# Two hybrid decoder layers on one Trainium2 core: high parts first in each weight half, and plain fp32 for the first pair of projections and the last down projections

## The chip, the core and the metric

The kernel runs on one core of a Trainium2 chip. The metric is the device time of one execution in microseconds. Besides the timed runs there is one profiled execution, from which every row below comes.

## What is computed

Two decoder layers work on 256 tokens of 1024 channels. Each layer projects `x` to 6,144 and more columns, runs three mixers on them (an RWKV-7 recurrence, a Conformer convolution, a short gated convolution), merges them with sigmoid gates, projects back and normalises. The first layer then has a dense SwiGLU, the second one a top-2-of-8 expert SwiGLU. Cut to what matters:

```python
p = x @ w_in                                   # all mixers' inputs and the gates
x = layernorm(alpha * x + (g_a*y_a + g_b*y_b + g_c*y_c) @ w_out)
f = (silu(x @ w_gate) * (x @ w_up)) @ w_down   # layer 0
...
yb = (silu(xs @ w_gate[e]) * (xs @ w_up[e])) @ w_down[e]   # layer 1, rows of expert e
x = layernorm(alpha * x + f)
```

## The kernel before

All weights come as 1 MB units of 128 partitions x 2048 fp32 columns, loaded on SyncE's queue (`fetch`, line 174) into a ring of buffers. Each unit is used in two halves of 1024 columns. `split` (line 197) makes two fp32r tiles of a half: ScalarE casts the high part `hi` (line 205), then VectorE subtracts it from the source to give the low part `lo` (line 207). Both tiles come from pools that turn round: three slots, to which a stage can add six.

A product is then made of several TensorE matmuls that add up in one PSUM tile. `mm3` (line 215) makes three of them: high x high (line 217), high x low (line 218) and low x high (line 219). `mm2` (line 1407) makes two, for experts whose rows are few: there the high and low parts of 64 rows lie side by side in one stationary tile, so `hi` (line 1408) and `lo` (line 1409) of the weights each need one pass.

In `proj` (line 360) the weights are stationary and `x` moves, 256 columns at a time, eight k-tiles to a half, so 24 matmuls. In the expert stage (`moe`, line 1190) the gathered rows are stationary and the weights move, 512 columns at a time. A half of a large expert then has two k-tiles (or, in a down projection, two output halves) and six matmuls, a half of a small one four. The four experts with most rows are `big`, with up to 128 rows, the other four are small, with up to 64. They run as two streams of steps `(r, j)`, rank `r` and 256 hidden columns `j` (0 to 10), in turn. A step has four halves of gate and up (`kind` 0) and, two steps later, two halves of the down projection (`kind` 1). The last two down steps of all are those of `(3, 10)` and `(7, 10)`. After the last down step of an expert, `scatter` (line 1309) casts and splits the result and adds it to the tokens by a one-hot matmul.

In the expert stage the order of TensorE, VectorE, ScalarE and SyncE is the order in which the program is written: for each half a cast, a subtraction, the matmuls, and then whatever is due from a list `later` (hidden activations, transposes, gathers, scatters). Everywhere else the compiler's scheduler orders the engines' queues.

At the start (`start`, line 340) unit 0 comes in two halves with `x` between them, `x` is split too (lines 356 and 357), and the first projected pair holds the inputs of the low-rank chain (`lora_part`, line 437): ScalarE shifts (line 428), tanh, sigmoids, exponentials. The mixer's own chain of small operations runs on VectorE and ScalarE, while `fill` (line 766) keeps TensorE in work with the other projections.

The kernel has matmuls on plain fp32 operands as well, in the mixer (lines 448, 459, 493). Each stands as two matmuls in the trace.

Of the kernel before, what the change touches and what calls it, by code (L numbers as in the profile page):

```python
# [11 lines left out]
F32 = mybir.dt.float32  # L12
F32R = mybir.dt.float32r
BF16 = mybir.dt.bfloat16
# [8 lines left out]
T = 256  # L23
# [25 lines left out]
BUSY = 7, 2, 4  # L49
LAG = 2  # L50
CONV_AT = 7
SPLITS = 3, 4, 0, 0, 3
# [91 lines left out]
class Net:  # L144
# [69 lines left out]

    def mm3(self, out, lh, ll, rh, rl, start, stop):
        mm = self.nc.tensor.matmul
        mm(out, lhsT=lh, rhs=rh, start=start, stop=False)  # L217
        mm(out, lhsT=lh, rhs=rl, start=False, stop=False)  # L218
        return mm(out, lhsT=ll, rhs=rh, start=False, stop=stop)  # L219

# [119 lines left out]
    def start(self):  # L340
        nc, A = self.nc, self.A
        raw = self.ring.tile([128, 2048], F32, name="raw")
        w = A["wst"][0]
        self.unit = 1
        with self.tc.tile_pool(name="xin", bufs=1) as xp:
            xf = xp.tile([128, 8, T], F32, name="xf")
            nc.sync.dma_start(raw[:, 0:1024], w[:, 0:1024])
            for g in range(2):
                nc.sync.dma_start(xf[:, 4 * g:4 * g + 4], A["xT"][:, 4 * g:4 * g + 4])
            nc.sync.dma_start(raw[:, 1024:2048], w[:, 1024:2048])  # L350
            self.first = [self.split(raw[:, 0:1024])]
            self.xTh = self.act.tile([128, 8, T], F32R, name="xTh")
            self.xTl = self.act.tile([128, 8, T], F32R, name="xTl")
            for g in range(2):
                s = slice(4 * g, 4 * g + 4)
                nc.scalar.copy(self.xTh[:, s], xf[:, s])  # L356
                nc.vector.tensor_sub(self.xTl[:, s], xf[:, s], self.xTh[:, s])  # L357
            self.first.append(self.split(raw[:, 1024:2048]))

    def proj(self, region, hl):  # L360
        hi, lo = hl
        for k in range(8):
            s = slice(k * 128, (k + 1) * 128)
            self.mm3(region, hi[:, s], lo[:, s], self.xTh[:, k], self.xTl[:, k], k == 0, k == 7)

    def by_token(self, hls, m):
        ps, n = self.pa(), 8 // len(hls)
        w, t = 1024 // n, slice(m * 128, (m + 1) * 128)
        for k in range(8):
            (hi, lo), s = hls[k // n], slice(k % n * w, (k % n + 1) * w)  # L370
            ins = self.mm3(ps[:, 0:w], self.xTh[:, k, t], self.xTl[:, k, t], hi[:, s], lo[:, s], k == 0, k == 7)
        return ps, ins
# [20 lines left out]

    def proj2(self):
        ps = self.pa()
        first, self.first = self.first, None
        for c, hl in enumerate(first or self.halves()):
            self.proj(ps[:, c * 256:(c + 1) * 256], hl)
        return ps
# [366 lines left out]
    def fill(self, l):  # L766
# [3 lines left out]
        with tc.tile_pool(name="fl", bufs=1) as W:  # L770
# [28 lines left out]
            for o in (yc, self.ybc):  # L799
# [4 lines left out]
                for hn, (hi, lo) in enumerate(self.halves()):  # L804
                    for n in range(0, 4, 2):
                        ps = self.pa()
                        for j in range(2):
                            for k in range(2):
                                s = slice(((n + j) * 2 + k) * 128, ((n + j) * 2 + k + 1) * 128)
                                self.mm3(ps[:, j * T:(j + 1) * T], hi[:, s], lo[:, s], yh[:, k], yl[:, k], k == 0, k == 1)  # L810
# [42 lines left out]
    def merge(self, l):  # L853
# [3 lines left out]
        for g in range(2):  # L857
            raw = self.fetch()
            for hn in range(2):
# [3 lines left out]
                for j in range(2):  # L863
                    for k in range(4):
                        s = slice((j * 4 + k) * 128, (j * 4 + k + 1) * 128)
                        self.mm3(ps[:, j * T:(j + 1) * T], hi[:, s], lo[:, s], self.yah[:, k], self.yal[:, k],
                                 k == 0, k == 3)
                s = slice(n, n + 2)
# [15 lines left out]
    def out_mm(self, lh, ll, hl, m, k, last, ns=(0, 1)):  # L884
        for n in ns:
            s = slice(n * 512, (n + 1) * 512)
            self.mm3(self.acc[2 * m + n], lh, ll, hl[0][:, s], hl[1][:, s], k == 0, k == last)

# [301 lines left out]
    def moe(self, W):  # L1190
# [33 lines left out]
        def due(t):  # L1224
            while True:
# [41 lines left out]
        def hidden_big(r, j, ps):  # L1267
# [4 lines left out]
            def turned():  # L1272
# [4 lines left out]

                def split():
                    hh = W.tile([128, 2, 128], F32R, name="hh", bufs=2)
# [7 lines left out]
        def hidden_small(r, j, ps):  # L1287
# [8 lines left out]
            def act():  # L1296
# [3 lines left out]

                def split():
                    hh = W.tile([128, 2, 128], F32R, name="hh", bufs=2)
                    nc.scalar.copy(hh[:, :, 0:64], sg)
# [30 lines left out]
        def product(kind, rj, i, hl):  # L1334
            r, j = rj
            big = r < BIG
            hi, lo = hl
            if kind == 0:
                if i == 0:
                    gps[rj] = self.pa()  # L1340
                ps = gps[rj]
                for kk in range(2):
                    k, s = 2 * i + kk, slice(kk * 512, (kk + 1) * 512)
                    if big:
                        self.mm3(ps, xe[r][:, 0, k], xe[r][:, 1, k], hi[:, s], lo[:, s], k == 0, k == 7)
                    else:
                        self.mm2(ps, xe[r][:, k], hi[:, s], lo[:, s], k == 0, k == 7)
                if i == 3:
                    del gps[rj]
                    at(4, lambda: (hidden_big if big else hidden_small)(r, j, ps))  # L1350
            else:
# [4 lines left out]
                if r not in Y:  # L1356
                    Y[r] = [self.pb(), self.pb()]
                for n in range(2):
                    s = slice(n * 512, (n + 1) * 512)
                    first, last = j == 0 and i == 0, j == NJ - 1 and i == 1  # L1360
                    h = hid[rj]
                    if big:
                        self.mm3(Y[r][n], h[0][:, i], h[1][:, i], hi[:, s], lo[:, s], first, last)
                    else:
                        self.mm2(Y[r][n], h[0][:, i], hi[:, s], lo[:, s], first, last)
                if i == 1:
# [39 lines left out]

    def mm2(self, out, l, rh, rl, start, stop):
        self.nc.tensor.matmul(out, lhsT=l, rhs=rh, start=start, stop=False)  # L1408
        self.nc.tensor.matmul(out, lhsT=l, rhs=rl, start=False, stop=stop)  # L1409

# [167 lines left out]
```

## Time and profile before

| | us |
|---|---|
| median of 3 runs (lowest, highest) | 1465.1 (1461.07, 1465.63) |
| profiled execution, its own time | 1463.08 |
| its span | 1461.3 |
| TensorE matmuls busy | 1405.8 |
| VectorE busy | 1223.5 |
| ScalarE busy | 970.0 |

The span is the time from the first to the last instruction of the profiled execution, the other 1.8 us lie around it. PE is TensorE's matmuls, PEld its weight loads, DVE VectorE, ACT ScalarE, POOL GpSimd. A matmul's recorded time includes waiting behind the one before it, so neighbouring matmuls overlap in the timeline; their pace is the distance between starts.

### The profile page before, as it was taken

What the parts mean: (1) busy time and instruction counts of PE and PEld (TensorE: products, weight loads), DVE (VectorE), ACT (ScalarE), POOL (GpSimd) and SP (SyncE); (2) the same over time, 40 slices, a digit from 0 to 9 for tenths busy, and PEclk for the clock granted to TensorE, in tenths of its full rate; (3) what the DMA queues carried; (4) which work ended last, traced back from release to release, by engine and by line L of the source; (5) the groups of instructions that cost most, each with busy time, mean ns of one, the idle gap of its engine ahead of it and who ended that gap; (6) DMA issues with size and microseconds to landing.
All of it is one profiled execution on the core that took longest, in us unless ns stands there. A gap on an engine that the chain in (4) does not pass through costs nothing.

```text
span 1461.3 us, 24189 instructions
## 1 busy us (share of the span) xinstructions
PE 1405.8 (96%) x9375; PEld 1202.3 (82%) x9377; DVE 1223.5 (84%) x1651; ACT 970.0 (66%) x1378; POOL 37.9 (3%) x72
## 2 busy tenths in 40 slices
PE   7999999999999999999999999999999999999994
PEld 6989898899997989999877887688876888768882
DVE  6799687755546799677789999999999999999997
ACT  7554564544435645464589888788887888878883
POOL 0030000000000030000000000000000000000000
PEclk9999999999999999999999999999999999999998
DMA  6334355655432424356389999899998999989990
GB/s 225 140 130 160 117 205 202 230 209 193 176 128 100 161 104 157 120 185 276 148 303 372 411 418 408 330 383 377 422 408 330 365 402 420 399 330 407 417 402 31
DMA packets 55640, 390.80 MB, mean 267 GB/s; under 512 B 6192, under 2 KB 6192, under 8 KB 9568
## 3 DMA queue, kind: packets, MB, share of 16 engines
q1 hardware_dynamic: 53136, 381.18, 67.0%
q0 software_dynamic: 2096, 7.49, 1.5%
q8 instruction: 75, 1.23, 0.3%
q10 hardware_dynamic: 288, 0.52, 0.1%
q14 instruction: 45, 0.37, 0.1%
HBM read 387.08 MB, written 2.10 MB: 266 GB/s over the span
## 4 chain that ended last, share of the span: by engine, by line
PE 79%; DVE 14%; ACT 3%; issue 3%; DMA 0%; ACTq 0%; DVEq 0%; POOLq 0%
PE pa L217 14%; PE pa L218 14%; PE pa L219 14%; DVE lo L207 7%; PE pb L218 5%; PE pb L219 5%; PE pb L217 5%; PE pa L1409 4%; PE pa L1408 4%; PE pa L1292 2%; PE pb L1409 2%; PE pb L1408 2%; ACT hi L205 2%; PE pb L627 1%; DVE ybc L230 1%
## 5 line engine op out<-in xcount | busy, mean ns | idle before, releaser
L207 DVE TENSOR_TENSOR lo<-raw,hi 128x1024 fp32r<-128x1024 f32 x648 | 775.5, 1229 | 126.8 <-ACT hi L205 125.8
L205 ACT CAST hi<-raw 128x1024 fp32r<-128x1024 f32 x648 | 656.3, 1052 | 175.9 <-PE pa L218 139.5
L217 PE MATMUL pa<-xTh,hi 128*128 128x256 f32 x1072 | 308.4, 288 | 7.3 <-ACT xTh L356 7.3
L219 PE MATMUL pa<-xTh,lo 128*128 128x256 f32 x1072 | 306.2, 286 | 6.1 <-DVE lo L207 6.1
L218 PE MATMUL pa<-xTl,hi 128*128 128x256 f32 x1072 | 304.6, 284 | 2.3 <-DVE xTl L357 2.3
L217 PEld LDWEIGHTS pa<-xTh,hi 128*128 128x128 f32 x1072 | 205.4, 192 | 11.8 <-ACT xTh L356 7.3
L219 PEld LDWEIGHTS pa<-xTh,lo 128*128 128x128 f32 x1072 | 205.4, 192 | 10.1 <-DVE lo L207 8.5
L218 PEld LDWEIGHTS pa<-xTl,hi 128*128 128x128 f32 x1072 | 205.9, 192 | 3.2 <-DVE xTl L357 2.6
L218 PE MATMUL pa<-lo,xeb 128*128 128x512 f32 x352 | 142.9, 406 | 4.1 <-DVE lo L207 3.2
L217 PE MATMUL pa<-hi,xeb 128*128 128x512 f32 x352 | 144.5, 410 | 0.0
L1408 PE MATMUL pa<-hi,xes 128*128 128x512 f32 x352 | 143.5, 408 | 0.7 <-ACT hi L205 0.7
L1409 PE MATMUL pa<-lo,xes 128*128 128x512 f32 x352 | 140.8, 400 | 2.9 <-DVE lo L207 2.9
L219 PE MATMUL pa<-hi,xeb 128*128 128x512 f32 x352 | 140.0, 398 | 0.0
L218 PE MATMUL pb<-lo,hh 128*128 128x512 f32 x264 | 105.2, 398 | 1.5 <-DVE lo L207 1.5
L217 PE MATMUL pb<-hi,hh 128*128 128x512 f32 x264 | 104.7, 397 | 0.0
L219 PE MATMUL pb<-hi,hl 128*128 128x512 f32 x264 | 104.4, 395 | 0.0
L207 DVE TENSOR_TENSOR lo<-ga,hi 128x1024 fp32r<-128x1024 f32 x74 | 88.3, 1222 | 3.7 <-ACT hi L205 3.7
L218 PEld LDWEIGHTS pa<-lo,xeb 128*128 128x128 f32 x352 | 66.9, 190 | 28.0 <-DVE lo L207 14.2
L1409 PEld LDWEIGHTS pa<-lo,xes 128*128 128x128 f32 x352 | 66.4, 189 | 21.8 <-DVE lo L207 8.8
L219 PEld LDWEIGHTS pa<-hi,xeb 128*128 128x128 f32 x352 | 66.8, 190 | 13.9
L217 PEld LDWEIGHTS pa<-hi,xeb 128*128 128x128 f32 x352 | 67.0, 190 | 13.5
L1408 PEld LDWEIGHTS pa<-hi,xes 128*128 128x128 f32 x352 | 66.3, 188 | 13.7 <-ACT hi L205 1.4
(394 smaller groups left out, 1993.4 us busy)
## 6 DMA issues: line engine op xcount, KB each, us to landing
raw<-in_wst SPq DMA_DIRECT2D x322, 1024.0 KB, 6.7
ga<-in_wst SPq DMA_DIRECT2D x37, 1024.0 KB, 7.1
raw<-in_wst SPq DMA_DIRECT2D x4, 512.0 KB, 6.7
xf<-in_xT SPq DMA_DIRECT2D x2, 512.0 KB, 5.6
raw<-in_lora SPq DMA_DIRECT2D x2, 512.0 KB, 5.5
kk<-in_lnp POOLq DMA_DIRECT2D x2, 512.0 KB, 4.0
v<-in_lnp POOLq DMA_DIRECT2D x2, 512.0 KB, 5.7
xsave<-ga POOLq DMA_DIRECT2D x2, 512.0 KB, 3.6
```

Of the source, the lines that this page charges most:

```text
L205: self.nc.scalar.copy(hi, src)
L207: self.nc.vector.tensor_sub(lo, src, hi)
L217: mm(out, lhsT=lh, rhs=rh, start=start, stop=False)
L218: mm(out, lhsT=lh, rhs=rl, start=False, stop=False)
L219: return mm(out, lhsT=ll, rhs=rh, start=False, stop=stop)
L230: return self.nc.vector.scalar_tensor_tensor(out, a, s, b, op0=op0, op1=op1)
L627: ins = nc.tensor.matmul(ps[s, n * 64:(n + 1) * 64], lhsT=lhsT[s, 8 * b + n], rhs=rhs[s, 8 * b + n], start=True, stop=True)
L1292: nc.tensor.matmul(pt[:, f * 64:(f + 1) * 64], lhsT=gu[:, f * 128:(f + 1) * 128], rhs=self.fold, start=True, stop=True)
L1408: self.nc.tensor.matmul(out, lhsT=l, rhs=rh, start=start, stop=False)
L1409: self.nc.tensor.matmul(out, lhsT=l, rhs=rl, start=False, stop=stop)
```

## The change

`mm3` and `mm2` take a list of products instead of one. For the whole list they first issue every matmul that reads the `hi` part of the weights, and then every one that reads `lo`. `moving` tells whether the weights are the moving or the stationary operand. `proj` gives its eight k-tiles as one list, the expert stage the two k-tiles or output halves of a half, and the merge, the branch outputs and `by_token` their lists alike.

The first pair of projections is not split any more: 16 plain fp32 matmuls read the loaded tiles. Fifteen matmuls on zeros (`WARM`) stand in front of them. The down projections of `(3, 10)` and `(7, 10)` are plain fp32 too, four matmuls of 512 columns each, without a cast and a subtraction of their weights.

```diff
+WARM = 15
-    def mm3(self, out, lh, ll, rh, rl, start, stop):
+    def mm3(self, items, moving):
         mm = self.nc.tensor.matmul
-        mm(out, lhsT=lh, rhs=rh, start=start, stop=False)
-        mm(out, lhsT=lh, rhs=rl, start=False, stop=False)
-        return mm(out, lhsT=ll, rhs=rh, start=False, stop=stop)
+        for out, lh, ll, rh, rl, start, _ in items:
+            mm(out, lhsT=lh, rhs=rh, start=start, stop=False)
+            if moving:
+                mm(out, lhsT=ll, rhs=rh, start=False, stop=False)
+            else:
+                mm(out, lhsT=lh, rhs=rl, start=False, stop=False)
+        for out, lh, ll, rh, rl, _, stop in items:
+            if moving:
+                ins = mm(out, lhsT=lh, rhs=rl, start=False, stop=stop)
+            else:
+                ins = mm(out, lhsT=ll, rhs=rh, start=False, stop=stop)
+        return ins
...
+            zero = xp.tile([128, 512], BF16, name="z")
+            nc.vector.memset(zero, 0.0)
+            ps = self.pa()
+            for _ in range(WARM):
+                nc.tensor.matmul(ps, lhsT=zero[:, 0:128], rhs=zero, start=True, stop=True)
...
-            self.first = [self.split(raw[:, 0:1024])]
+            ps = self.first = self.pa()
+            for c in range(2):
+                for k in range(8):
+                    s = slice(c * 1024 + k * 128, c * 1024 + (k + 1) * 128)
+                    nc.tensor.matmul(ps[:, c * T:(c + 1) * T], lhsT=raw[:, s], rhs=xf[:, k], start=k == 0, stop=k == 7)
...
-            self.first.append(self.split(raw[:, 1024:2048]))
...
+        plain = [(r, NJ - 1) for r in (BIG - 1, NE - 1)]
...
+                    if (r, j) in plain:
+                        hh = W.tile([128, 2, 128], F32, name="hh", bufs=2)
+                        nc.gpsimd.memset(hh[:, :, 64:128], 0.0)
+                        nc.scalar.copy(hh[:, :, 0:64], sg)
+                        hid[r, j] = (hh,)
+                        return
...
+                if lo is None:
+                    for n, s in ns:
+                        nc.tensor.matmul(Y[r][n], lhsT=h[0][:, i], rhs=hi[:, s], start=first, stop=last)
+                elif big:
+                    self.mm3([(Y[r][n], h[0][:, i], h[1][:, i], hi[:, s], lo[:, s], first, last)
+                              for n, s in ns], True)
+                else:
+                    self.mm2([(Y[r][n], h[0][:, i], hi[:, s], lo[:, s], first, last) for n, s in ns])
...
-                hl = self.split(raw[:, h * 1024:(h + 1) * 1024])
-                product(kind, rj, i, hl)
+                part = raw[:, h * 1024:(h + 1) * 1024]
+                product(kind, rj, i, (part,) if kind and rj in plain else self.split(part))
...
+    def mm2(self, items):
+        for out, l, rh, rl, start, _ in items:
+            self.nc.tensor.matmul(out, lhsT=l, rhs=rh, start=start, stop=False)
+        for out, l, rh, rl, _, stop in items:
+            self.nc.tensor.matmul(out, lhsT=l, rhs=rl, start=False, stop=stop)
```

## Rows read from the trace of the kernel before

**Rows 1.** The page: span, and busy time of the engines.

```profile
span 1461.3 us, 24189 instructions
...
PE 1405.8 (96%) x9375; PEld 1202.3 (82%) x9377; DVE 1223.5 (84%) x1651; ACT 970.0 (66%) x1378; POOL 37.9 (3%) x72
```

**Rows 2.** Waits: who waited for whom, us in total, times, longest us.

```profile
ACT hi L205 <- PE pa L218: 139.5, 77, 4.0
...
PE pb L1409 <- DVE lo L207: 6.4, 9, 2.1
PE pa L219 <- DVE lo L207: 6.1, 8, 1.6
PE pa L218 <- DVE lo L207: 3.2, 10, 0.4
PE pa L1409 <- DVE lo L207: 2.9, 5, 0.8
PE pb L218 <- DVE lo L207: 1.5, 3, 0.8
```

**Rows 3.** Windows of the expert stage: length, busy PE, PEld, DVE, ACT, POOL; clock, DMA.

```profile
820.00:895.00 75.00, 75.00 (x347) 61.15 (x347) 73.58 (x80) 64.84 (x85) 0.00 (x0) 1.00 1.01 415
896.00:1000.00 104.00, 100.66 (x466) 78.68 (x464) 97.05 (x113) 83.08 (x121) 0.00 (x0) 1.00 0.95 366
```

**Rows 4.** The chain that ended last, first 64 us: start, us, what.

```profile
10.14 0.58 PE pa L218
...
13.71 0.21 PE pa L218
...
17.57 0.12 PE pa L218
...
57.78 1.82 PE pb L493 x8
```

**Rows 5.** ScalarE's timeline of the start: start, us, line, operation, [idle before <-releaser].

```profile
6.18 1.04 ACT L356 CAST xTh<-xf 128x1024 fp32r<-128x1024 f32 x1 [0.42 <-DMA xf<-in_xT]
...
9.34 1.04 ACT L205 CAST hi<-raw 128x1024 fp32r<-128x1024 f32 x1 [0.27 <-DMA raw<-in_wst]
...
13.13 1.05 ACT L205 CAST hi<-raw 128x1024 fp32r<-128x1024 f32 x1 [2.74 <-DMA raw<-in_wst]
...
17.84 0.47 ACT L428 ACTIVATE sh<-pa,par 128x255 f32<-128x255 f32 x1 [1.95 <-PE pa L219]
...
29.30 1.03 ACT L205 CAST hi<-raw 128x1024 fp32r<-128x1024 f32 x1
```

**Rows 6.** Timeline of the mixer in layer 0, around its last wait for lo.

```profile
108.15 1.05 ACT L205 CAST hi<-raw 128x1024 fp32r<-128x1024 f32 x1
...
110.72 0.38 PE L219 MATMUL pa<-xTh,lo 128*128 128x256 f32 x1 [0.97 <-DVE lo L207]
```

**Rows 7.** TensorE's timeline in the expert stage, at the first change of experts.

```profile
946.36 0.39 PE L217 MATMUL pa<-hi,xeb 128*128 128x512 f32 x1
947.02 0.50 PE L218 MATMUL pa<-lo,xeb 128*128 128x512 f32 x1 [0.28 <-DVE lo L207]
947.36 0.39 PE L219 MATMUL pa<-hi,xeb 128*128 128x512 f32 x1
947.59 0.40 PE L217 MATMUL pa<-hi,xeb 128*128 128x512 f32 x1
```

**Rows 8.** Timeline of the last down projections and scatters.

```profile
1432.34 0.39 PE L217 MATMUL pb<-hi,hh 128*128 128x512 f32 x1
...
1436.13 0.40 PE L219 MATMUL pb<-hi,hl 128*128 128x512 f32 x1
...
1439.16 0.40 PE L1408 MATMUL pb<-hi,hh 128*128 128x512 f32 x1
1441.69 0.50 PE L1409 MATMUL pb<-lo,hh 128*128 128x512 f32 x1 [2.14 <-DVE lo L207]
1443.37 1.07 ACT L1316 CAST yh<-pb 128x512 fp32r<-128x512 f32 x2 [4.32 <-PE pb L1409]
```

More of the change, by code (lines that the diff above doesn't have):

```diff
@@ L357, in start @@
                 nc.vector.tensor_sub(self.xTl[:, s], xf[:, s], self.xTh[:, s])
-            self.first.append(self.split(raw[:, 1024:2048]))
     def proj(self, region, hl):
         hi, lo = hl
-        for k in range(8):
-            s = slice(k * 128, (k + 1) * 128)
-            self.mm3(region, hi[:, s], lo[:, s], self.xTh[:, k], self.xTl[:, k], k == 0, k == 7)
+        cols = [slice(k * 128, (k + 1) * 128) for k in range(8)]
+        self.mm3([(region, hi[:, s], lo[:, s], self.xTh[:, k], self.xTl[:, k], k == 0, k == 7)
+                  for k, s in enumerate(cols)], False)
     def by_token(self, hls, m):
@@ L368, in by_token @@
         w, t = 1024 // n, slice(m * 128, (m + 1) * 128)
-        for k in range(8):
-            (hi, lo), s = hls[k // n], slice(k % n * w, (k % n + 1) * w)
-            ins = self.mm3(ps[:, 0:w], self.xTh[:, k, t], self.xTl[:, k, t], hi[:, s], lo[:, s], k == 0, k == 7)
+        for h, (hi, lo) in enumerate(hls):
+            ins = self.mm3([(ps[:, 0:w], self.xTh[:, h * n + i, t], self.xTl[:, h * n + i, t],
+                             hi[:, i * w:(i + 1) * w], lo[:, i * w:(i + 1) * w], h + i == 0, h * n + i == 7)
+                            for i in range(n)], True)
         return ps, ins
@@ L394, in proj2 @@
     def proj2(self):
+        first, self.first = self.first, None
+        if first is not None:
+            return first
         ps = self.pa()
-        first, self.first = self.first, None
-        for c, hl in enumerate(first or self.halves()):
+        for c, hl in enumerate(self.halves()):
             self.proj(ps[:, c * 256:(c + 1) * 256], hl)
@@ L807, in fill @@
                         for j in range(2):
-                            for k in range(2):
-                                s = slice(((n + j) * 2 + k) * 128, ((n + j) * 2 + k + 1) * 128)
-                                self.mm3(ps[:, j * T:(j + 1) * T], hi[:, s], lo[:, s], yh[:, k], yl[:, k], k == 0, k == 1)
+                            w = [slice(((n + j) * 2 + k) * 128, ((n + j) * 2 + k + 1) * 128) for k in range(2)]
+                            self.mm3([(ps[:, j * T:(j + 1) * T], hi[:, s], lo[:, s], yh[:, k], yl[:, k], k == 0, k == 1)
+                                      for k, s in enumerate(w)], False)
                         r = o[:, 4 * hn + n:4 * hn + n + 2].rearrange("p a t -> p (a t)")
@@ L863, in merge @@
                 for j in range(2):
[L864 to L867, printed above, removed]
+                    w = [slice((j * 4 + k) * 128, (j * 4 + k + 1) * 128) for k in range(4)]
+                    self.mm3([(ps[:, j * T:(j + 1) * T], hi[:, s], lo[:, s], self.yah[:, k], self.yal[:, k],
+                               k == 0, k == 3) for k, s in enumerate(w)], False)
                 s = slice(n, n + 2)
@@ L884, in out_mm @@
     def out_mm(self, lh, ll, hl, m, k, last, ns=(0, 1)):
-        for n in ns:
-            s = slice(n * 512, (n + 1) * 512)
-            self.mm3(self.acc[2 * m + n], lh, ll, hl[0][:, s], hl[1][:, s], k == 0, k == last)
+        cols = [slice(n * 512, (n + 1) * 512) for n in ns]
+        self.mm3([(self.acc[2 * m + n], lh, ll, hl[0][:, s], hl[1][:, s], k == 0, k == last)
+                  for n, s in zip(ns, cols)], True)
     def ln_rows(self, idx, pool, names=("lnG", "lnB")):
@@ L1301, in split @@
                 def split():
+                    if (r, j) in plain:
+                        hh = W.tile([128, 2, 128], F32, name="hh", bufs=2)
+                        nc.gpsimd.memset(hh[:, :, 64:128], 0.0)
+                        nc.scalar.copy(hh[:, :, 0:64], sg)
+                        hid[r, j] = (hh,)
+                        return
                     hh = W.tile([128, 2, 128], F32R, name="hh", bufs=2)
@@ L1336, in product @@
             big = r < BIG
-            hi, lo = hl
+            hi, lo = hl if len(hl) == 2 else (hl[0], None)
             if kind == 0:
@@ L1341, in product @@
                 ps = gps[rj]
[L1342 to L1347, printed above, removed]
+                ks = [(2 * i + kk, slice(kk * 512, (kk + 1) * 512)) for kk in range(2)]
+                if big:
+                    self.mm3([(ps, xe[r][:, 0, k], xe[r][:, 1, k], hi[:, s], lo[:, s], k == 0, k == 7)
+                              for k, s in ks], True)
+                else:
+                    self.mm2([(ps, xe[r][:, k], hi[:, s], lo[:, s], k == 0, k == 7) for k, s in ks])
                 if i == 3:
@@ L1357, in product @@
                     Y[r] = [self.pb(), self.pb()]
[L1358 to L1365, printed above, removed]
+                first, last, h = j == 0 and i == 0, j == NJ - 1 and i == 1, hid[rj]
+                ns = [(n, slice(n * 512, (n + 1) * 512)) for n in range(2)]
+                if lo is None:
[4 more added lines that the diff above has]
+                              for n, s in ns], True)
+                else:
+                    self.mm2([(Y[r][n], h[0][:, i], hi[:, s], lo[:, s], first, last) for n, s in ns])
                 if i == 1:
@@ L1405, in moe @@
             due(1 << 30)
-    def mm2(self, out, l, rh, rl, start, stop):
-        self.nc.tensor.matmul(out, lhsT=l, rhs=rh, start=start, stop=False)
-        self.nc.tensor.matmul(out, lhsT=l, rhs=rl, start=False, stop=stop)
+    def mm2(self, items):
[3 more added lines that the diff above has]
+            self.nc.tensor.matmul(out, lhsT=l, rhs=rl, start=False, stop=stop)
     def spill(self, W, base, after):
```

1 line of the change is left out of this document (added).

## The prediction

> **What bounds the kernel now.** I read the page first. TensorE is busy for 1405.8 of 1461.3 us [rows 1], so 55.5 us at most are to be had from waits, if its matmuls stay as they are. The waits view then tells what TensorE waits for: five groups, 20.1 us together, name one producer, VectorE's subtraction that makes `lo` [rows 2]. TensorE waits for `lo` and hardly ever for `hi`, because `lo` is `hi` plus one more operation. The windows show where: in steady expert steps TensorE has no idle time, with VectorE busy for 73.58 of 75 us, but around a change of experts 3.3 of 104 us are idle [rows 3]. The timelines show single waits. At 947.02 a matmul waits for `lo`; starts go 946.36, 947.02, 947.36, where two paces of 0.23 would do [rows 7]. So 0.54 us are lost, though 0.28 stand as idle: the weight load that is otherwise hidden is paid too. The 20.1 us are therefore a lower figure of the loss.
>
> **The order inside a half.** No matmul is added or removed by it; `lo` is needed later. In a large expert's half the first reader of `lo` moves from place 2 to place 5 of six, in a small one's from 2 to 3 of four, in a projection's from 3 to 17 of 24. Where VectorE sets the time of `lo`, the gain of a run of waits is not their sum: TensorE that no longer stands at the first one reaches the next one sooner. The gain is what is left to do after the last late `lo`: two matmuls in place of five (3 x 0.23 = 0.7 us), two in place of three (0.23), or 8 in place of 22 (14 x 0.12 = 1.7), and never more than the waits lost.
>
> *Expert stage.* A change of experts occurs three times with the same pattern. Each has three runs of waits that end in a large half (0.7 us each; the one at 947.02 [rows 7] closes the third) and one single wait, taken as large as the one shown, 0.54 us: 2.6 us, times three is 7.9. The opening, with the gathers, ends in a small half (0.2) and has one more such single wait (0.5). Together 8.6 us. Bounds: nothing, if VectorE merely makes TensorE wait elsewhere; all that is lost there, which by starts is about twice the idle time of 3.3 us per change, so 3 x 6.3 plus some 5 at the opening, 24.
>
> *Mixers.* The last late `lo` comes at 110.72, after 0.97 us of idle time [rows 6]; layer 1 repeats it. Its `hi` is cast by 109.2 [rows 6]. From there 24 matmuls of 0.12 end at 112.1, against 110.72 + 22 x 0.12 = 113.4 before. I take 1.2 us per layer, 2.4 in all; bounds 0 and all waits of that kind, 9 by starts (6.1 as idle [rows 2]).
>
> **The start.** Removed: two casts, two subtractions, 48 fp32r matmuls. Added: 15 matmuls on zeros and 16 plain ones. Of plain fp32 the chain shows eight recorded matmuls, four products of 256 columns, in 1.82 us [rows 4]: 0.455 a product, with fill. At first TensorE ran at 0.21 us per matmul, later at 0.12 [rows 4]: the lower level of 1.2 GHz, left for 2.4 GHz after it had run without gaps from 10.14 on. The zeros have 512 columns, so 0.43 at the lower level, and 6.4 us if all run there. They start near 1.3 (after a small memset, an estimate) and end by 7.7. The first half of x is there at 6.18, the last weights at 9.34 [rows 5]. I take 7.0 for the first plain product: 16 x 0.455 = 7.3, end at 14.3, between 13.5 and 15.0. Before, ScalarE's first shift came at 17.84 [rows 5], so 3.5 us sooner.
>
> Not all of it stays. The next unit lands at 13.13 either way and its `hi` is ready at 14.18 [rows 5], so TensorE goes on at once. But in the trace ScalarE cast two halves ahead while it waited for the first pair; then it ran the low-rank chain until 29.30 [rows 5]. Now the second of those casts falls into that chain and delays it by 1.05. I take 2.5 us; bounds 0 (all casts behind the chain) and 4.3.
>
> The Trainium skill (TensorE: Matmul & The Clock Gate, Part 1) says that the moment at which the clock changes differs from run to run of one kernel. By that the zeros might all run slowly and end at 7.7; the first pair would then end at 15.0 and the start give 1.8 instead of 2.5. One profile can't show this.
>
> **The end.** The last two down steps lose four casts and four subtractions. Their products of 512 columns have no row; I take twice 0.455, so 0.91, 3.64 us a step. The split steps cost 12 and 8 matmuls of 0.23, that is 2.8 and 1.9, so TensorE's work grows by 2.6 us. But the waits go: `(3, 10)` took 1432.34 to 1436.53, and `(7, 10)` 1439.16 to about 1443.8, with 2.14 us idle [rows 8]. Two late halves in front give 0.23 each, so `(3, 10)` starts at 1431.9 and ends at 1435.7, with pipeline drain 0.8 sooner. The scatter between keeps its time, `(7, 10)` starts at 1438.3 and ends at 1442.1. Its first output half is finished 0.9 before the second, so the last cast starts near 1442.1, against 1443.9 (second of two from 1443.37 [rows 8]). That is 1.8, and the chain behind it is unchanged: I take 1.9, bounds 0.9 and 2.9 (0.43 to 0.5 per recorded matmul). The memset on GpSimd and the shorter hidden split lie beside these matmuls. If that cover went, the memset would add under 0.3 (as VectorE's and GpSimd's small fills, an estimate).
>
> **The sum.** 8.6 + 2.4 + 2.5 + 1.9 = 15.4 us off the profiled execution's 1463.1, so 1447.7. That execution stood 2.0 below the median of 1465.1, which gives 1449.7; I say 1450.
>
> **Rivals.** *VectorE is the bound, not the order.* It is busy 98% of steady expert steps [rows 3]; then `lo` comes when it comes, the changes of experts and mixers give nothing, and 4.4 us are left: 1460.7. Against it: in those same windows TensorE has no idle time at all, and VectorE has 7 us free of the 104 at a change [rows 3]. Chance 0.15.
>
> *The zeros don't do what they are for.* If the clock still stood at the lower level during the plain products, 16 x 0.91 = 14.6 us from 7.7 on end at 22.3, 4.5 later than before; with the rest this gives 1465.1 - 12.9 + 4.5 = 1456.7. For it: the level is low at first [rows 4]. Against: TensorE then works without a gap from 1.3 on. Chance 0.10.
>
> *Slots of `lo` come free too late; slower.* `hi` of a large half is now free after place 4, `lo` after 6, one place later than before. ScalarE's casts already wait 139.5 us for TensorE to free slots [rows 2]. If a subtraction began to wait as well, each of a large step's six halves would cost VectorE 0.23, 1.4 us per pair of steps of 15 us. VectorE has 1.42 us free in 75 [rows 3], 0.3 per pair. The other 1.1 over 39 pairs are 43 us, so 1465.1 - 15.4 + 43 = 1493. It decides from the point at which `lo` lags `hi` by more than the cast in between, 1.05 us [rows 5]. The lag is 2 x 0.23 = 0.47 here and 8 x 0.12 = 0.96 in a projection, close but below. Chance 0.05.
>
> **How the numbers follow.** The forecast has 0.70. Its own range is 1440 to 1458: the low end where most of the waits lost in the expert stage go, the high end where half of it is taken back. The 8-in-10 range takes in the second rival and half of the first: 1440 to 1460. A measurement of this kernel tells about 0.3%, 4.4 us, from no change, so faster means below 1460.7. The first rival lies on that bound (0.07 faster, 0.08 same), the second gives 0.09 and 0.01, the forecast 0.69 and 0.01: faster 0.85, same 0.10, slower 0.05.
>
> **What would show it.** Right: idle time before readers of `lo` near 947 and 110 is gone or shorter, a change of experts takes some 2.6 us less, ScalarE's first shift comes near 14.3, recorded plain matmuls of 512 columns start 0.45 apart, and `(7, 10)` has no gap inside. Wrong: the same idle time before the later matmul, plain products at 0.9 at the start, a gap in TensorE while ScalarE runs the low-rank chain, or VectorE waiting for TensorE in front of a subtraction. The forecast fails if the scheduler, outside the expert stage, orders the queues otherwise.

## The result and the profile after

The changed kernel takes 1447.6 us (median of 4 runs, 1447.15 to 1449.57), the kernel before 1464.4 in the runs beside it. The medians lie 16.8 us apart. The ratio of the runs, as it was recorded, is 0.9893, with a 95% interval from 0.9876 to 0.9910, which is 15.7 us; below, too, a difference beside a ratio is worked out from it. I had forecast 1450.0 (1440 to 1460). The profiled execution took 1447.3 and its span is 1445.5, 15.8 below the span before [rows 1].

The sum came out. Its terms did not all: the expert stage and the end gave a little more than they were priced at, the mixers nearly nothing, and 1.7 us of the difference between the two profiles are the clock's: TensorE's clock fell to its lower level for a short time in each, at different places. That is what the experiments had to separate. In what follows *before* and *after* are the two kernels, and kernel 1 to 11 those of the experiments.

The page of after, span and busy time:

```profile
span 1445.5 us, 24195 instructions
...
PE 1403.7 (97%) x9372; PEld 1201.2 (83%) x9372; DVE 1213.3 (84%) x1644; ACT 965.7 (67%) x1372; POOL 38.1 (3%) x73
```

TensorE's busy time fell by 2.1 us and the span by 15.8. What went is idle time: 41.8 us now against 55.5 [rows 1]. The waits view of after has the names (us in total, times, longest):

```profile
PE pb L1445 <- DVE lo L208: 3.8, 8, 0.7
PE pa L219 <- ACT hi L206: 3.6, 4, 1.2
...
PE pa L1445 <- DVE lo L208: 2.1, 5, 0.5
PE pb L702 <- DVE r L674: 2.0, 4, 0.6
...
PE pa L223 <- DVE ysl L246: 1.4, 2, 0.7
...
PE pa L226 <- DVE lo L208: 0.3, 1, 0.3
```

The five groups that waited for `lo` came to 20.1 us [rows 2]. Now three are left, 6.2 us. But three other lines are new or larger: 3.6 us for `hi`, 2.0 for `r`, 1.4 for `ysl`. They are what the mixers wait for now.

Windows of the expert stage (length, busy PE, PEld, DVE, ACT, POOL; clock, DMA), moved by the 5 us that the kernel is ahead here:

```profile
815.00:890.00 75.00, 75.00 (x348) 61.16 (x347) 73.53 (x80) 64.90 (x85) 0.00 (x0) 1.00 1.01 417
891.00:995.00 104.00, 102.24 (x481) 81.67 (x480) 99.50 (x115) 85.78 (x126) 0.00 (x0) 1.00 0.96 377
```

The steady steps are as they were [rows 3]. At the change of experts TensorE is idle for 1.76 us of 104 instead of 3.34, and VectorE does 99.50 us of work in that time instead of 97.05: the stage is pulled together. The idle time that went is 1.6 us, the time won 3.1 (below). The stall at 947.02 [rows 7] had cost 0.54 us for 0.28 of idle time in the same way; that it is the weight load that makes up the rest was not tested. TensorE's timeline at the end of that change:

```profile
936.45 0.63 PE L1445 MATMUL pa<-lo,xes 128*128 128x512 f32 x2
936.91 0.63 PE L1443 MATMUL pb<-hi,hh 128*128 128x512 f32 x2
937.83 0.73 PE L1445 MATMUL pb<-lo,hh 128*128 128x512 f32 x2 [0.29 <-DVE lo L208]
938.40 0.62 PE L1443 MATMUL pb<-hi,hh 128*128 128x512 f32 x2
```

The wait in the large half at 947.02 [rows 7] is gone; the last one left, 0.29, is in a small half. The timeline of the start, TensorE and ScalarE:

```profile
1.20 6.17 PE L360 MATMUL pa<-z 128*128 128x512 bf16 x15 [1.20 <-DVE z L357]
...
7.21 7.07 PE L370 MATMUL pa<-xf,raw 128*128 128x256 f32 x32
...
15.85 1.08 PE L469 MATMUL pb<-Ls,raw 64*64 64x256 f32 x8 [1.14 <-DVE Ls L240]
...
14.31 0.47 ACT L449 ACTIVATE sh<-pa,par 128x255 f32<-128x255 f32 x1 [5.11 <-PE pa L370]
14.69 1.04 ACT L206 CAST hi<-raw 128x1024 fp32r<-128x1024 f32 x1
...
19.21 1.04 ACT L206 CAST hi<-raw 128x1024 fp32r<-128x1024 f32 x1
...
20.87 1.06 ACT L206 CAST hi<-raw 128x1024 fp32r<-128x1024 f32 x1
...
27.59 1.03 ACT L206 CAST hi<-raw 128x1024 fp32r<-128x1024 f32 x1
```

The first shift stands at 14.31, where 14.3 was forecast, against 17.84 [rows 5]. All casts of the next units now stand behind that shift. The first comes at 14.69, so that its `hi` is ready at 15.73, and TensorE, with nothing to do until `Ls`, the input of the low-rank products, stands idle for 1.14 us. Two more fall deeper into the low-rank chain, at 19.21 and 20.87. In the trace of before one cast, at 18.76, stands between the first shift and the end of the chain; now there are three. So the cast behind the chain comes at 27.59 against 29.30: 3.53 us won at the pair are 1.71 there. The mixer of layer 0:

```profile
105.74 0.38 PE L219 MATMUL pa<-xTh,hi 128*128 128x256 f32 x1 [1.23 <-ACT hi L206]
...
144.84 0.33 PE L702 MATMUL pb<-RH,r 64*64 64x64 f32 x4 [0.46 <-DVE r L674]
145.74 0.45 PE L702 MATMUL pb<-RH,r 64*64 64x64 f32 x8 [0.57 <-DVE r L674]
...
187.38 0.39 PE L223 MATMUL pa<-ysl,hi 128*128 128x256 f32 x1 [0.68 <-DVE ysl L246]
```

The wait for `lo` at 110.72 [rows 6] is gone, but one for `hi` stands in its place, and later come waits that the trace before has shorter or not at all. The end, both plain steps and the last casts:

```profile
1418.28 3.60 PE L1394 MATMUL pb<-raw,hh 128*128 128x512 f32 x8
...
1424.51 3.60 PE L1394 MATMUL pb<-raw,hh 128*128 128x512 f32 x8
...
1427.28 0.59 ACT L1348 CAST yh<-pb 128x512 fp32r<-128x512 f32 x1 [4.78 <-PE pb L1394]
1428.14 0.59 ACT L1348 CAST yh<-pb 128x512 fp32r<-128x512 f32 x1 [0.27 <-PE pb L1394]
```

A plain step has no gap inside and takes 8 x 0.43 us and some 0.16 at its end. The last cast, the second of two from 1443.37 [rows 8], starts at 1428.14.

**Clock.** The two profiles differ in one thing that is no part of the change: the times at which TensorE's granted clock fell from 2.4 GHz (1.00 in the windows) to 1.2 GHz (0.50). Windows of before (the number after POOL's count is the granted clock):

```profile
704.00:714.00 10.00, 9.68 (x75) 8.26 (x74) 7.99 (x37) 4.99 (x9) 0.00 (x0) 1.00 0.29 105
714.00:720.50 6.50, 6.50 (x22) 5.54 (x21) 5.70 (x5) 6.17 (x9) 0.00 (x0) 0.50 0.30 91
```

and of after:

```profile
191.00:201.00 10.00, 10.00 (x68) 8.03 (x67) 9.17 (x11) 4.31 (x6) 0.00 (x0) 1.00 0.33 115
201.50:204.50 3.00, 3.00 (x16) 3.00 (x15) 2.53 (x4) 2.98 (x6) 0.38 (x1) 0.50 0.65 270
...
714.00:720.00 6.00, 6.00 (x30) 4.91 (x30) 4.81 (x4) 5.47 (x8) 0.00 (x0) 1.00 0.41 134
```

In before the clock stands at 1.2 GHz for 6.8 us from 713.9, although TensorE was busy for 9.68 of the 10 us ahead of it; in after for 3.4 us from 201.4, out of 10 us without idle time. So each profile carries a loss at another place, and shifts have to be read on either side of them.

### The profile page after: what moved, and what is told of

Same layout as the page of the kernel before. It is cut to its first block, busy times and chain, and to the rows that moved or that the text cites. A ratio compares the mean times of both kernels' runs of the same rounds, so it can differ in the third digit from the quotient of the medians.

```text
span 1445.5 us, 24195 instructions
## 1 busy us (share of the span) xinstructions
PE 1403.7 (97%) x9372; PEld 1201.2 (83%) x9372; DVE 1213.3 (84%) x1644; ACT 965.7 (67%) x1372; POOL 38.1 (3%) x73
## 4 chain that ended last, share of the span: by engine, by line
PE 78%; DVE 16%; ACT 3%; issue 3%; ACTq 0%; DVEq 0%
PE pa L219 13%; PE pa L223 7%; PE pa L228 7%; DVE lo L208 7%; PE pa L226 6%; PE pa L221 6%; PE pb L221 5%; PE pb L219 5%; PE pb L226 5%; PE pa L1445 5%; PE pa L1443 4%; PE pb L1445 3%; DVE cv L240 3%; PE pa L1318 2%; PE pb L1443 2%
## 5 line engine op out<-in xcount | busy, mean ns | idle before, releaser
L208 DVE TENSOR_TENSOR lo<-raw,hi 128x1024 fp32r<-128x1024 f32 x642 | 767.3, 1225 | 135.9 <-ACT hi L206 135.3
L219 PE MATMUL pa<-xTh,hi 128*128 128x256 f32 x1056 | 265.1, 288 | 3.6 <-ACT hi L206 3.6
L223 PE MATMUL pa<-xTl,hi 128*128 128x256 f32 x1056 | 259.8, 283 | 0.0
L228 PE MATMUL pa<-xTh,lo 128*128 128x256 f32 x1056 | 149.2, 284 | 0.0
L228 PEld LDWEIGHTS pa<-xTh,lo 128*128 128x128 f32 x1056 | 136.9, 192 | 0.2
L1443 PE MATMUL pa<-hi,xes 128*128 128x512 f32 x352 | 114.9, 407 | 0.7 <-ACT hi L206 0.7
L1445 PE MATMUL pa<-lo,xes 128*128 128x512 f32 x352 | 112.2, 399 | 2.2 <-DVE lo L208 2.1
L226 PE MATMUL pa<-lo,xeb 128*128 128x512 f32 x352 | 111.9, 399 | 0.8 <-DVE lo L208 0.3
L226 PE MATMUL pb<-lo,hh 128*128 128x512 f32 x260 | 82.5, 396 | 0.1
L206 ACT CAST hi<-ga 128x1024 fp32r<-128x1024 f32 x74 | 75.4, 1055 | 0.0
```

The costliest lines, as they stand in the source:

```text
L206: self.nc.scalar.copy(hi, src)
L208: self.nc.vector.tensor_sub(lo, src, hi)
L226: ins = mm(out, lhsT=lh, rhs=rl, start=False, stop=stop)
L228: ins = mm(out, lhsT=ll, rhs=rh, start=False, stop=stop)
```

## The experiments

Medians of runs that spread by 3 us or more don't separate terms of 2 us; traces do. A **shift** below is the start of one and the same TensorE instruction in a kernel's trace minus its start in the trace of before; negative is ahead. The marks are first instructions behind a stage, with their time in before. Kernels whose start was not touched stand 0.3 to 0.6 us late already at 58 us, so steps from mark to mark count, not the levels.

| mark (us in before) | after | order everywhere (1) | order in experts (4) | start (2) | end (3) | large halves (9) |
|---|---|---|---|---|---|---|
| end of layer 0 (449.3) | -0.53 | +0.71 | +0.36 | -2.74 | +0.62 | +0.42 |
| router (700.6) | -1.05 | +0.38 | +0.58 | -2.68 | +0.64 | +0.42 |
| behind the clock's fall (724.0) | -4.21 | -2.76 | +0.57 | -5.84 | -2.51 | -2.74 |
| ahead of the first change of experts (880) | -4.97 | -3.53 | -0.33 | -5.82 | -2.50 | -3.24 |
| behind it (1030) | -8.06 | -6.61 | -3.42 | -5.79 | -1.62 | -5.87 |
| behind the second (1205) | -11.18 | -9.69 | -6.51 | -4.98 | -1.63 | -6.97 |
| behind the third (1381) | -13.52 | -12.02 | -8.85 | -4.97 | -1.63 | -8.84 |
| end of the span | -15.79 | -12.93 | -9.59 | -5.05 | -3.42 | -9.17 |

Between 700.6 and 724.0 all kernels of the table but one gain 3.15 us, the one with the start alone too, whose expert stage is that of before. That is the fall of the clock at 713.9, which the trace of before has and theirs have not; the kernel with the order in the experts alone fell at the same place and gains nothing.

**1. The order alone.** The first pair split as before, no plain steps:

```diff
-WARM = 15
-        plain = [(r, NJ - 1) for r in (BIG - 1, NE - 1)]
+        plain = []
-            ps = self.first = self.pa()
...
+            self.first = [self.split(raw[:, 0:1024])]
```

> Only the order of the products is changed (high parts first, in every call of mm3 and mm2); the start and the last down projections are those of before. Theory: the order is worth what the expert stage shows, about 9 us there (.75 at its opening and 3.1, 3.1 and 2.3 at the three changes of experts, by the shifts between the two traces), and what it saves in the mixers (about 1 us in each layer) is given back before the layer ends, where VectorE's chain sets the pace; so 1455 us against 1464.4. Rival 1, the mixers keep their gain: 2.4 more, 1453. Rival 2, the gain of the expert stage was mostly the clock, which fell at 714 us in the trace of before and not in that of after: then about 4 us, 1460, and the changes of experts show less than 1.5 us each.

Measured: 1452.5 us, ratio 0.9929 (0.9913 to 0.9945), 10.4 us. By time alone rival 1's 1453 fits better than the theory's 1455, but the granted clock was higher in these six runs (0.9948 on average, against 0.9936 in the 23 of before beside them), and the trace decides. It has no fall of the clock ahead of the one in its last 10 us. The three changes give 3.08, 3.08 and 2.33 us (third column), the opening 0.77, the end another 0.9. At the router nothing is left of the mixers: it is 0.38 late, and was 0.34 late at 58 us. The second rival, that the expert stage's gain is the clock's, is out.

**2. The start alone.** mm3 and mm2 in the order of before, no plain steps:

```diff
-        for out, lh, ll, rh, rl, start, _ in items:
+        for out, lh, ll, rh, rl, start, stop in items:
             mm(out, lhsT=lh, rhs=rh, start=start, stop=False)
...
+            mm(out, lhsT=lh, rhs=rl, start=False, stop=False)
+            ins = mm(out, lhsT=ll, rhs=rh, start=False, stop=stop)
```

> Only the start is changed (15 products of zeros, then the first pair of projections as plain fp32); the products keep the order of before, and the last down projections are split. Theory: the first shift ends 3.5 us earlier, some 3 us of it are still there at 60 us, and at the end of layer 0 (445 us) less than 1.5 are left, because VectorE's subtraction and the wait for ysl do not move with TensorE; 1463 us. Rival 1, the start keeps what it wins: 2.5 to 3 us at 445 us too, 1461.5. Rival 2, nothing is won at all, because the low rank chain behind it waits for the later casts: 1464.4. A fall of the clock moves any of these by 1.7 or 3.4 us; it is read from the windows.

Measured: 1462.0 us, ratio 0.9991 (0.9980 to 1.0001). My theory fell and rival 1 held: the shift is -2.7 at 58 us and still -2.68 at the router. What the start wins it keeps. So it was not the start that was given back in the changed kernel.

**3. The end alone.**

```diff
-WARM = 15
+        plain = [(r, NJ - 1) for r in (BIG - 1, NE - 1)]
```

> Only the last down projections are plain fp32 (16 columns blocks of two regions, 512 wide); start and order are those of before. Theory: 1.9 to 2.3 us, all of it between the last yh and the last store, 1462.3 us. Rival: without the new order the split products would have been covered less, so that the plain form is worth more here, 3 us, 1461.4.

Measured: 1461.3 us, ratio 0.9984 (0.9972 to 0.9997), 2.3 us; by the shift 1.8 us, all between the third change and the end, just under the theory's 1.9. By the trace the rival's 3 is out; the interval of the times, 0.4 to 4.1 us, does not exclude it. Order alone (0.9) and plain steps alone (1.8) overlap somewhat: together they give 2.3 in after.

**4. The order in the expert stage alone.** All calls of mm3 outside it take the three products block by block again:

```diff
+    def mm3_old(self, items, moving):
...
-        self.mm3([(region, hi[:, s], lo[:, s], self.xTh[:, k], self.xTl[:, k], k == 0, k == 7)
+        self.mm3_old([(region, hi[:, s], lo[:, s], self.xTh[:, k], self.xTl[:, k], k == 0, k == 7)
```

> As the run with the order alone, but with the new order inside the expert stage only; the projections, the output projections and the low rank steps of both layers run the three products per block one behind the other as before. Theory: the same time as with the order everywhere, within 1 us: about 1455. Rival 1, the mixers keep their gain: 2.4 us slower than the order everywhere. The shift at the end of layer 1 (711 us) against before tells it without the clock: theory 0, rival -2.4 in the other kernel.

Measured: 1452.9 us, ratio 0.9929 (0.9912 to 0.9946), the same ratio as with the order everywhere. At the router the two stand 0.19 apart, without a fall of the clock in either up to there. The layers' new order is worth 0.2 us, not 2.4. The two layers differ: in layer 0 it loses 0.35 (+0.71 against +0.36 at 449.3), in layer 1 it wins 0.54. At the end of layer 0 it costs something of its own: the two output halves of the last down projection now end within one matmul of each other, VectorE's first sum of them starts at 443.76 in place of 443.31 in kernel 4, and TensorE waits 0.44 us for what follows from it at 449.97, where kernel 4 does not wait.

**5 and 6. Where the mixers' gain goes.** Kernels 1 and 4 again, each with 20 of the depthwise convolution's 30 multiply-adds per channel block left out, so that VectorE has less to do:

```diff
-                for j in range(1, 31):
+                for j in range(1, 11):
```

> The kernel with the order alone, and of the depthwise convolution's 30 multiply-adds per channel block only 10 are done (the other 20 are left out), so VectorE has 40 x 0.41 = 16 us less work per layer between 553 and 595 us. It is read against the next run, by the shift of its matmuls. Theory: the projections' order wins about 2 us by the end of the projections (565 us), and VectorE, which is busy without a break until 595, gives it back through the subtraction that makes r; with the break in VectorE's work the shift between the two kernels, 0 at 710 us, stays at 1 us or more. Rival 1: the waits for lo were there only because VectorE was full of those multiply-adds, so that with fewer of them neither order waits: no shift at 565 and none at 710. Rival 2: the gain is lost behind 595 whatever VectorE does, at ScalarE and at ysl: a shift of 1 to 2 us at 565 and none at 710.

> The pair of the run before: the new order in the expert stage alone, and the same 20 of 30 multiply-adds of the depthwise convolution left out. Both should be faster than their full kernels by some us per layer if VectorE's chain sets the pace there; by nothing if TensorE does.

Measured: 1450.6 and 1455.6 us, one run each; only the shifts are read. With the whole convolution, TensorE's waits in the timeline of layer 1, order everywhere:

```profile
551.76 0.39 PE L218 MATMUL pa<-xTh,hi 128*128 128x256 f32 x1 [1.19 <-ACT hi L205]
...
590.89 0.33 PE L691 MATMUL pb<-RH,r 64*64 64x64 f32 x4 [0.47 <-DVE r L663]
591.79 0.56 PE L691 MATMUL pb<-RH,r 64*64 64x64 f32 x12 [0.57 <-DVE r L663]
...
700.97 0.39 PE L1059 MATMUL pa<-rt,a 128*128 128x8 f32 x2 [0.24 <-ACT a L949]
```

and order in the experts alone:

```profile
554.11 0.39 PE L235 MATMUL pa<-xTh,lo 128*128 128x256 f32 x1 [0.96 <-DVE lo L207]
...
701.16 0.39 PE L1067 MATMUL pa<-rt,a 128*128 128x8 f32 x2 [0.24 <-ACT a L957]
```

The new order wins 2.3 us by the end of the projections. Then come waits for two other results of VectorE: 1.04 us for `r`, of the recurrence, where the other kernel has none, and 0.68 for `ysl`, the low part of the short convolution's output, where the other has 0.16. With the short convolution, order everywhere:

```profile
552.12 0.39 PE L218 MATMUL pa<-xTh,hi 128*128 128x256 f32 x1 [1.19 <-ACT hi L205]
...
701.49 0.74 PE L1059 MATMUL pa<-rt,a 128*128 128x8 f32 x4 [0.24 <-ACT a L949]
```

and order in the experts alone:

```profile
554.50 0.39 PE L235 MATMUL pa<-xTh,lo 128*128 128x256 f32 x1 [0.96 <-DVE lo L207]
...
703.04 0.74 PE L1067 MATMUL pa<-rt,a 128*128 128x8 f32 x4 [0.24 <-ACT a L957]
```

The waits for `r` are gone, and at the router the new order is 1.55 us ahead. The clock of both fell at 647 us; that of the first also fell at 203, which cost 1.49 us in the pair of traces that shows it alone (after and kernel 7, between 188 and 208 us). Without that fall, and without the 0.47 us by which the first is ahead already at 58 us, the lead is 2.6 us for both layers, against 0.2 with the whole convolution. In layer 1 alone 2.3 were won by the end of the projections, all of it still there behind them, and 1.8 at the router. So the theory held: VectorE, without a break in its queue from 560 to 590 us (29.96 of 30 busy), is what takes most of the gain back, through `r`. The wait for `ysl` stays with the short convolution, 0.69 us, and takes the other part. Rival 1 is out: `lo` at 554.50 is as late with the short convolution, 0.96 us. So is rival 2, by which nothing would be left at the router.

Kernel 6 shows the other half. With the old order, 40 multiply-adds less per layer win next to nothing: between 58 us and the router its shift goes from +0.96 to +2.46, of which 1.50 are the step at the fall at 647; kernel 4 goes from +0.32 to +0.58 there, so the short convolution gives 0.3 us. TensorE behind `lo` and VectorE's queue end at nearly the same time, and either alone is shortened for almost nothing. The `hi` at 551.76 waits for a cast that stands in ScalarE's queue behind four copies of 2.51 us together, which themselves waited 5.97 us for VectorE.

**7 and 8. The zeros.**

```diff
-WARM = 15
+WARM = 1
```

> As the changed kernel, but with 1 product of zeros in place of 15. Theory: the zeros are there for the clock; without them TensorE starts the plain products near 6.3 us, when x is there, at the lower clock of 1.2 GHz (0.43 per recorded matmul in place of 0.216); the clock rises some 5.5 us after that, as it rose 5.5 us after the zeros began. So about 13 of 32 recorded matmuls run at 0.43 and 19 at 0.216: 9.7 us, end at 16.0 in place of 14.3, and 1.7 us of the start's 2.7 are lost. Rival: the products wait for the last weights at 9.3 us anyway, so that the zeros give less than 0.5 us: end at 14.8 or sooner.

and with `WARM = 12`:

> As the changed kernel, but with 12 products of zeros. In the changed kernel the zeros ran at 0.43 until 6.72 us and ended at 7.2, while x had landed near 6.2. Theory: the zeros end near 6.4, the plain products start there, two of their recorded matmuls still run at the lower clock, and all of them end near 13.8, 0.5 us sooner, unless one of them then waits for its weights. Rival: the weights, the last of which land at 9.3 us, hold them up: gaps in TensorE between 6.4 and 9.5 us and the same end at 14.3. Either way under 0.6 us, less than the median can show.

Measured: 1448.1 us (1445.94 to 1450.88; ratio 0.9892) and 1451.2 us (1445.58 to 1452.47; ratio 0.9900), neither to be told from the changed kernel. TensorE's timeline with 1 zero:

```profile
6.43 9.21 PE L370 MATMUL pa<-xf,raw 128*128 128x256 f32 x32 [4.62 <-DMA xf<-in_xT]
```

and ScalarE's:

```profile
13.38 1.99 ACT L206 CAST hi<-raw 128x1024 fp32r<-128x1024 f32 x2 [4.25 <-DMA raw<-in_wst]
...
16.59 0.46 ACT L449 ACTIVATE sh<-pa,par 128x255 f32<-128x255 f32 x1
```

The plain products took 9.21 us instead of 7.07, about as the theory had it: the clock rose at 10.61 us, 4.2 after they began. And yet the layer then ran 0.8 us ahead of the changed kernel, from 27 us to 188, against both sides of the expectation. A reason to test lies in ScalarE's queue: with 1 zero both casts of the second unit stand in front of the first shift, and none of them falls into the low-rank chain. With 12 zeros the plain products began at 6.30 and took 7.51, the first shift came at 13.84, and the layer ran 0.3 behind. When the pair ends is not what sets the layer's start.

**9. Large halves alone.** New order in mm3 of the expert stage, mm2 as before:

```diff
-        for out, l, rh, rl, start, _ in items:
+        for out, l, rh, rl, start, stop in items:
...
-        for out, l, rh, rl, _, stop in items:
```

> New order in the large experts' halves alone (six products, mm3); the small experts' halves (four products, mm2) and both layers keep the order of before. By the working of the prediction a change of experts gets 3 x 0.7 = 2.1 us of its gain from runs of waits that end in a large half, and the rest, one single wait, may lie in either kind: so 2.1 to 2.6 of the 3.1 us that the order everywhere gave, and none of the opening's 0.8. Rival: a large expert's halves hold only part of the waits, and TensorE meets the next late lo in a small half instead: under 1.5 us per change.

Measured, one run: 1453.9 us beside 1463.1. The changes give 2.63, 1.10 and 1.87 us (last column); the clock fell at 1100.4, inside the second, which cost 0.8 us in the kernel with the start alone, whose clock fell at 1100.9. So the large halves hold 80 to 85% of a change where nothing disturbs, at the upper end of the theory's 2.1 to 2.6. It missed the opening, where they gave 0.5 of 0.8. Waits for `lo` in small halves of this kernel:

```profile
PE pb L1441 <- DVE lo L207: 7.2, 9, 2.1
...
PE pa L1441 <- DVE lo L207: 3.6, 8, 0.8
```

10.8 us, against 9.3 before [rows 2] and 5.9 in after: without the new order in the small halves TensorE stands longer at their `lo`.

**10 and 11. Casts in front of the shift.** The changed kernel, with the second unit split before the first shift is queued, and the shift held behind that cast:

```diff
         if first is not None:
+            self.ready = list(self.halves())
+            self.wait = self.cast
             return first
-        for c, hl in enumerate(self.halves()):
+        ready, self.ready = self.ready, None
+        for c, hl in enumerate(ready or self.halves()):
...
+            with ExitStack() as es:
+                if self.wait is not None:
+                    es.enter_context(tc.issue_after(self.wait.ins))
+                    self.wait = None
+                nc.scalar.activation(t[:, 1:T], ps[:, 0:T - 1], AF.Copy, scale=self.p(l, "mu", ct))
```

> The changed kernel with both casts of the second unit of weights put in front of the first shift in ScalarE's queue (all 15 zeros kept). In the run with 1 zero the first pair ended 1.4 us later than in the changed kernel and yet the layer ran 0.8 us ahead of it from 27 us on; there both casts stood in front of the shift. Theory: ScalarE's place for the second cast is what the start pays, so here the casts run 13.3 to 15.3, the shift follows at 15.4, 1.2 us sooner than with 1 zero, and the layer runs some 2 us ahead of the changed kernel from 30 us to the end of layer 0: 1445.5 us. Rival: the lead of the run with 1 zero came from something else in its queues (TensorE's order of low rank products and second pair), so that with this cast order the shift of the layer is 0 or of the other sign.

> The same with 1 product of zeros in place of 15. Theory: the plain products end at 15.6 as in the run with 1 zero, the casts at 15.3, so the zeros are worth only the 0.3 us between the two and what the transposes behind the products add: at most 1.2 us behind the run with 15 zeros. Rival: the order of the casts, not the zeros, is the same in both, and the two stand within 0.3 us at 100 us.

ScalarE's timeline of kernel 10:

```profile
12.00 1.99 ACT L206 CAST hi<-raw 128x1024 fp32r<-128x1024 f32 x2 [2.91 <-DMA raw<-in_wst]
14.08 0.58 ACT L324 COPY hsT<-pb 8x512 f32<-8x512 f32 x1
14.57 0.46 ACT L458 ACTIVATE sh<-pa,par 128x255 f32<-128x255 f32 x1
```

Both casts end ahead of the shift, which is only 0.26 us later than in the changed kernel. TensorE begins the second pair at 13.80, without the 1.14 us of idle time at 15.85 in after, and from 41 us to 182 the layer runs 2.4 us ahead. The low-rank chain itself ends no sooner (its last exponential starts at 26.62, in after at 26.64); what is won is weights that are ready. Not all of it is the casts': the clock rose at 5.47 us here and at 6.82 in after, so that the plain products end 0.67 us sooner (13.61 against 14.28). Without that at least 1.7 us are left, near the theory's 2, and the rival is out. With 1 zero the lead is 0.65: under this cast order the zeros are worth 1.8 us, more than the 1.2 allowed, again with the early rise in it. Kernel 10 takes 1446.6 us (1445.93 to 1449.63; ratio 0.9893, 0.9867 to 0.9920), kernel 11 1448.1 (ratio 0.9904). Kernel 10 has the shortest time of all. The four runs alone do not resolve 2 us, but each run's mean granted clock is on record. Over the 38 runs of before beside the experiments, the time grows by 1.25 us with each 0.001 that this clock is lower, from 1460.6 at 0.997 to 1466.9 at 0.990, and keeps to that line within 1.4 us. Brought to the same clock by this slope, an estimate, kernel 10 is 2.3 us ahead of after.

## Why the prediction was right, and where it was not

*Expert stage, 8.6 us:* right. Three changes gave 3.09, 3.12 and 2.34 in after (8.55 for 7.9), the opening 0.76 (for 0.7). The rule behind it, that a run of waits saves only the matmuls left behind the last late `lo`, held in size: kernel 9, with the new order in large halves alone, gives 2.6 where three large halves and the single wait were priced at that. The waits were not followed one by one, so the rule is borne out by its sums only. Twice the idle time, the upper bound of 24, was far off.

*End, 1.9 us:* right, 1.8 alone and 2.3 with the order. A plain product of 512 columns took 2 x 0.43 = 0.86 us, the lower end of the bounds; 0.91 was taken. No gap stands in front of either plain step, so the memset on GpSimd cost nothing.

*Start, 2.5 us:* right in size, by a path that was only in part as written. The shift at 14.31 was forecast to 0.01. But "its `hi` is ready at 14.18 [rows 5], so TensorE goes on at once" did not come: that cast went behind the shift as well, and TensorE stood idle for 1.14 us. And behind the first shift the chain now takes in three casts where it had one: two more, for 1.82 us, and not one for 1.05. Kernel 10, with the first two casts in front of the shift, shows what this was worth. In layer 0 the kernel was 2.3 ahead at 58 us, 2.7 in kernel 2. The difference goes with the clock: kernel 2 had 2.4 GHz from 5.19 us on and began the plain products at 6.40, after had it from 6.82 and began them at 7.21. The prediction gave 1.8 to that side. In four kernels that all begin their zeros at 1.20 the clock rose at 5.19, 5.47, 6.82 and 7.04 us. The Trainium skill (TensorE: Matmul & The Clock Gate, Part 1) says that the moment differs from run to run. These traces agree.

*Mixers, 2.4 us:* wrong, and this is the step that failed: "From there 24 matmuls of 0.12 end at 112.1, against 110.72 + 22 x 0.12 = 113.4 before. I take 1.2 us per layer, 2.4 in all". The projections' gain was even larger, 2.3 us a layer, but I priced it where it arises and not where it is read. I had written that bound as "0 and all waits of that kind", and named no work behind the projections that could end later than TensorE. The rival *VectorE is the bound* was the right thought at the wrong place: I argued it from the expert stage, where it doesn't hold, and not from the mixer, where VectorE's queue runs without a break behind the projections. Of 2.4 us 0.2 came; with a shorter queue on VectorE (kernels 5 and 6) 2.6 stay.

*Not priced:* falls of the clock. It fell in before at 713.9 for 3.15 us of loss and in after at 201.4 for 1.49, which is 1.66 us in favour of after. Start 2.3, mixers 0.2, experts 9.3, end 2.3 and clock 1.7 make the 15.8 us between the spans; the forecast's 15.4 held because those falls and the small excess of experts and end stood in for the mixers. That the sum came so close is luck; without the clock the traces give 14.1. In the comparison of all runs, 15.7, falls happen on both sides. By the slope of experiment 10 the four runs of after (0.9940 on average, against 0.9934 in the 38 of before) owe some 0.7 us to the clock, an estimate, as the runs of before beside them have no clock on record. Single parts by their ratios (order 10.4, start 1.3, end 2.3) come to 14.0.

The rival of the lower clock at the start is out (32 recorded plain matmuls in 7.07 us in after), and so is the one of late slots of `lo`: VectorE's busy share of a steady step is unchanged.

## What to carry to other kernels

If the second half of a split operand is late, issue all that reads the first half before anything that reads the second. Price it by what is left behind the last late piece, and then ask which engine's queue ends next: a gain on TensorE that another engine's full queue absorbs is worth next to nothing, though the waits it removed are really gone. Where two results of one list are read by another engine in turn, the new order makes the first of them later. Read terms of 2 us from the start of the same instruction in two traces, on both sides of every fall of the clock, and put conversions on a busy engine's queue before a dependent chain rather than into it.

## What was not expected of the hardware

The clock's falls are frequent here and come at few places. Thirteen profiles show 17 falls to 1.2 GHz ahead of the one in which each kernel ends, and all lie near 201 to 203, 453 to 458, 644 to 648, 710 to 716, 923 or 1100 us; which of them happen differs between executions, and the kernel with the order alone had none. No long idle time stands ahead of them: in the 10 us ahead of twelve of them TensorE was busy for 9.67 to 10.00 us, ahead of the other five (453 to 458, 923 and 1100) for 7.5 to 8.6, with no single wait over 0.93 us. What makes the clock fall there is not shown. Their price differs by place: 6.8 us at half speed cost 3.15 us at 714, 3.4 us cost 1.49 at 201, but 0.8 at 1100 and 923, inside changes of experts, where TensorE waits for VectorE anyway.
